# The experts' first pair read tile by tile in turn, a fixed order on TensorE, and a reordered router chain

## The chip, the core and the metric

The kernel runs on one core of one Trainium2 chip. The metric is device time in microseconds (us) of one execution; 0.2% of it is about 2.4 us. An execution that was profiled has two numbers: its own device time, and the span from its first to its last profiled instruction.

The engines are named as in the profile: PE is TensorE's matmuls, PEld its weight loads, DVE is VectorE, ACT is ScalarE, POOL is GpSimd, SP is SyncE, which here issues the large loads from HBM. SBUF is the on-chip memory that tiles are loaded into, PSUM the one that matmuls write.

## What is computed

One decoder layer for 256 tokens of width 2048, all in float32. First a mixer: RMSNorm, one wide input projection, three branches (pooling, sparse attention, cross-attention), gates and an output projection that is added to x. Then the part that matters here, a mixture of experts on the RMSNorm of the new x:

```python
lg = h @ w_router_group                      # 4 groups, top-1
le = (h @ w_router_expert).reshape(.., 4, 4) # 4 experts a group, top-2 of the chosen group
w  = pg_top * pe_top / sum(pe_top)           # from two softmaxes
a  = einsum('bsd,edf->bsef', h, w_e_gate)    # 16 experts, 2048 -> 512
b  = einsum('bsd,edf->bsef', h, w_e_up)
act = silu(a) * b * combine                  # combine is w, 0 for experts not chosen
x  = x + einsum('bsef,efd->bsd', act, w_e_down)
```

The reference multiplies every token with every expert. The kernel multiplies each expert with the tokens that chose it, up to 64 in a round; a loop after the last pair repeats the rounds where an expert has more.

## The kernel before

**Up to the residual.** The mixer takes the first 600 us and is not touched. The output projection runs in four column blocks `n` of 512; each ends in two residual tiles (token halves `t` = 0, 1) that DVE adds to `x2` (L815). `route_in` (L785 on) then transposes such a block on PE (L790), copies it to SBUF as `xt` (ACT, L792; one buffer), squares it for the norm (L793) and multiplies it with the router weights. For n < 3 these go into `rps`; for n = 3 they go straight into `rl` (L802), the PSUM tile with the 20 router values of each token.

**The router chain.** `Rc` is a copy of `rl` (L872). DVE ranks groups and experts by comparisons (L875 to L882), which gives the mask `msk`; three small matmuls (L886 to L888) count the tokens ahead of each one, and `slot` (L889) is its place with its expert. The chain of norm and softmax (`r2`, `E`, `cmb`, `cwf`, `cw`; L890 to L916) gives the weights. `warm(n, ...)` (L282) issues n matmuls of the identity whose result is not used; an f32 matmul is two instructions in the trace.

**Gathering.** Experts come in pairs (`pair(pr, ...)`, eight of them), and two pairs share one `Gather` of four experts. Its `sel` (L931) is a 0/1 matrix made from `slot`. A `step()` multiplies two 128-row blocks of x, each split into a high and a low part `xs` (ACT copy L949, DVE subtraction L950, three buffers), with `sel` (eight matmuls, L966) and DVE writes the result, scaled, to `xg` (L967). There are eight steps. `back()` transposes `sel` into `selT` for the way back and makes the factors `fac` of each token.

**A pair.** 24 weight tiles of 1 MB each: 8 of gate, 8 of up, 8 of down. `gemm` runs the 8 gate tiles into the PSUM tile `ag`, then the 8 up tiles into `au`; a tile is four f32 matmuls, eight instructions (L1006). Sigmoid (ACT) and two DVE products (L1028, L1030) give `sg`, four transposes (L1035) and a copy (L1037) give `aT`, and the eight down tiles follow (L1075), two to an output block `ad` of 512 columns. `scatter` splits `ad` into `ob` (ACT L1045, DVE L1046) and multiplies it back to the tokens with `selT` (L1051, four matmuls for both token halves); DVE adds the result to `y` (L1053). The steps of the next `Gather` are called between the tiles of the odd pair's down part; in the first pair they are called by `ahead_` in the gate gemm.

**What sets the order.** A scheduler orders each engine's instructions by a simulated timeline; `keep_in_program_order` ties one to what was traced before it on its engine. In `gemm` the first pair's gate matmuls and gather steps are tied (by `pe`, which is why the trace shows them under L991), its up matmuls are not, nor, but for `warm`, is anything else on PE in this part. SP's loads are all tied (L190), in the order of `todo`.

**The buffers of the weight tiles.** The first 18 tiles go, during the output projection, into buffers that earlier parts leave: 4 `hq` (trace name `wh`), 6 `ex` (`we`), and in turn `raw` (`wr`) and `mx` (`wm`). Two more, the tiles in `late`, go to a pool of their own once the router is done. From then on 16 buffers rotate in the fixed order hq x4, ex x6, raw, mx, raw, mx, raw, raw: each load waits until PE has finished with the tile that lay in its buffer, and all loads behind it on SP wait too. Counting loads from 0, number 20 is the first that waits for the experts' part, and number k from 36 on takes the buffer of number k - 16. Numbers 24 to 47 are pair 1, and so on; number 191 is the last tile, which is loaded in two halves.

Of the kernel before, what the change touches and what calls it, by code (L numbers as in the profile page):

```python
# [20 lines left out]
P = 128  # L21
# [32 lines left out]
def layer_kernel(tc, x, xT, memT, pos, cst, band, gains, bgate, wmem, wxq, widx, wkqvp, wpg, wgb, wo, wr, we, out):  # L54
# [671 lines left out]
    todo = deque((pr, i) for pr in range(NE // 2) for i in range(24))  # L726
    late = [(0, 6), (0, 7)]
# [55 lines left out]
    rl = sm_tile([P, NT, 20], "rl")  # L783

    def route_in(n, t, ac):  # L785
        owp = pools["ow"][1]
        sl = x2[:, t, n * 512 : (n + 1) * 512]
        ps = sm_tile([P, 4, P])
        for kk in range(4):
            nc.tensor.transpose(ps[:, kk], sl[:, kk * P : (kk + 1) * P], ident)  # L790
        xt = owp.tile([P, 4, P], F32, tag="xt", name="xt")
        A.activation(xt, ps, AF.Copy)  # L792
        A.activation(ac, sl, AF.Square, accum_out=ss2[:, t, n : n + 1])  # L793
        yield
        if n < 3:

            for kk in range(4):
                mm(rps[32 * kk : 32 * kk + 32, t * P : (t + 1) * P], wrt[:, 4 * n + kk], xt[:, kk],
                   start=n == 0 and t == 0, stop=n == 2 and t == 1)
        else:  # L800
            for kk in range(4):
                mm(rl[:, t], xt[:, kk], wrt[:, 4 * n + kk, 0:20], start=False, stop=t == 1 and kk == 3)  # L802
        yield
        if n == 2 and t == 1:
            lgT = owp.tile([P, S], F32, tag="xt", name="lgT")
            V.tensor_copy(lgT, rps)
            yield
            for u in range(NT):
                mm(rl[:, u], lgT[:, u * P : (u + 1) * P], cs[:, C_SUM : C_SUM + 20], start=u == 0, stop=False)
            yield  # L810

    for n in range(4):
        def odone(t, ac, n=n):
            sl = x2[:, t, n * 512 : (n + 1) * 512]
            V.tensor_add(sl, sl, ac)  # L815
            bg.append(route_in(n, t, ac))
# [15 lines left out]

    wps = acc_tile("warm")
    warm(7, ident, P, wps)
# [7 lines left out]
    for j, w in enumerate(late):  # L842
        et = pools["x"][1].tile([P, 4, 512], F32, name="we%d" % j)
        load(et, we[w])
        ahead.insert(w[1], et)
# [26 lines left out]
    V.tensor_copy(Rc, R.rearrange("p t g e -> p (t g) e"))  # L872
    vi = Rc.unsqueeze(3).to_broadcast(C)
    vj = Rc.unsqueeze(2).to_broadcast(C)
    V.tensor_tensor(c2, vj, vi, op=ALU.is_equal)  # L875
    V.tensor_tensor(c1, vj, vi, op=ALU.is_gt)
    V.tensor_mul(c2, c2, cs[:, C_TIE : C_TIE + 16].rearrange("p (i j) -> p i j", j=4).unsqueeze(1).to_broadcast(C))
    V.tensor_add(c1, c1, c2)
    V.tensor_reduce(rank.rearrange("p t g e -> p (t g) e"), c1, axis=AX.X, op=ALU.add)
    V.tensor_scalar(ohg, rank[:, :, 0], 0.0, None, op0=ALU.is_equal)  # L880
    V.scalar_tensor_tensor(m4[:, 0], rank[:, 0, 1:5], 1.5, ohg[:, 0].unsqueeze(2).to_broadcast([P, 4, 4]), op0=ALU.is_lt, op1=ALU.mult)
    V.scalar_tensor_tensor(m4[:, 1], rank[:, 1, 1:5], 1.5, ohg[:, 1].unsqueeze(2).to_broadcast([P, 4, 4]), op0=ALU.is_lt, op1=ALU.mult)  # L882
# [3 lines left out]
    mm(ps[:, 0], ut, msk[:, 0], start=True, stop=True)  # L886
    mm(ps[:, 1], ones, msk[:, 0], start=True, stop=False)
    mm(ps[:, 1], ut, msk[:, 1], start=False, stop=True)  # L888
    V.tensor_mul(slot, ps, msk)  # L889
# [3 lines left out]

    m1 = rt([P, NT, 5], "m1")
    tc.keep_in_program_order(V.tensor_reduce(m1, R, axis=AX.X, op=ALU.max))
# [3 lines left out]
    warm(2, ident, P, wps)  # L899
    gs = rt([P, NT], "gs")  # L900
    tc.keep_in_program_order(V.tensor_reduce(gs, E[:, :, 0], axis=AX.X, op=ALU.add))

    tc.keep_in_program_order(V.tensor_mul(cmb.rearrange("p t (g e) -> p t g e", e=4), E[:, :, 1:5], m4))
# [14 lines left out]
    gf = cs[:, C_GFFN : C_GFFN + KD]  # L918
    ys_ = []
    EQ = 4  # L920
    SQ = EQ * 64

    class Gather:

        def __init__(self, q, slot_, first=False):
            self.q = q
            self.pe = pe if first else mm
            self.sel = wk.tile([P, NT, EQ, 64], F32R, tag="sel", name="sel")  # L930
            V.tensor_tensor(  # L931
                self.sel,
                cs[:, C_IOTA : C_IOTA + 64].unsqueeze(1).unsqueeze(1).to_broadcast([P, NT, EQ, 64]),
                slot_[:, :, EQ * q : EQ * q + EQ].unsqueeze(3).to_broadcast([P, NT, EQ, 64]),
                op=ALU.is_equal)
            self.flat = self.sel.rearrange("p t e s -> p t (e s)")
            self.xg = None
            self.parts = deque()
            self.next = 0
            self.todo = deque(range(KD // 2))  # L940

        def split(self):
            if self.next == KD:
                return
            k = self.next
            self.next += 1
            xs = wk.tile([P, 2, NT, P], F32R, tag="xs", name="xs", bufs=3)
            src = x2[:, :, k * P : (k + 1) * P]
            A.activation(xs[:, 0], src, AF.Copy)  # L949
            V.tensor_sub(xs[:, 1], src, xs[:, 0])  # L950
            self.parts.append(xs)

        def step(self):
            if not self.todo:
                return
            b = self.todo.popleft()
            if self.xg is None:
                self.xg = wk.tile([P, KD, SQ], F32, tag="xg", name="xg")
            ps = sm_tile([P, 2, SQ])
            for kk in range(2):  # L960
                while len(self.parts) < 2 and self.next < KD:
                    self.split()
                xs = self.parts.popleft()
                for t in range(NT):
                    for h in range(2):
                        self.pe(ps[:, kk], xs[:, h, t], self.flat[:, t], start=t + h == 0, stop=t + h == 2)  # L966
            V.tensor_mul(self.xg[:, 2 * b : 2 * b + 2], ps, gf[:, 2 * b : 2 * b + 2].unsqueeze(2).to_broadcast([P, 2, SQ]))  # L967

        def back(self, wp):

            self.selT = wp.tile([P, 2, S], F32R, tag="selT", name="selT", bufs=2)
            ps = sm_tile([P, 2, NT, P])
            for h in range(2):
                for t in range(NT):
                    nc.tensor.transpose(ps[:, h, t], self.flat[:, t, h * P : (h + 1) * P].bitcast(F32), ident)
            A.activation(self.selT, ps.rearrange("p h t q -> p h (t q)"), AF.Copy)
            ps = sm_tile([P, 2, 18])
            for h in range(2):
                for t in range(NT):
                    for u in range(2):  # L980
                        mm(ps[:, h], self.flat[:, t, h * P : (h + 1) * P], cw[:, u, t], start=t + u == 0, stop=t + u == 2)
            self.f = wp.tile([P, 2, 2], F32, tag="fac", name="fac", bufs=2)
            for h in range(2):
                V.tensor_copy(self.f[:, h, 0:1], ps[:, h, NE : NE + 1])
                for e in range(2):
                    c = EQ * self.q + 2 * h + e
                    V.tensor_copy(self.f[64 * e : 64 * e + 64, h, 1:2], ps[64 * e : 64 * e + 64, h, c : c + 1])

    def pe(*a, **k):

        tc.keep_in_program_order(mm(*a, **k))  # L991

    def pair(pr, slot_, base, store, ga, first=False):
        hf = pr % 2

        def gemm(mm_, step=None):
            ac = acc_tile("gu")
            for i in range(8):
                if step:
                    step(i)  # L1000
                w = wtile()
                for kk in range(2):
                    k = 2 * i + kk
                    for e in range(2):
                        s0 = hf * P + 64 * e
                        mm_(ac[64 * e : 64 * e + 64], ga.xg[:, k, s0 : s0 + 64], w[:, 2 * kk + e],  # L1006
                            start=k == 0, stop=k == KD - 1)
                if i == late[-1][1] and "x" in pools:
                    close(pools.pop("x")[0])
                    pools["w2"] = pool("work2", side="right")  # L1010
            return ac

        def ahead_(i):

            while 8 - len(ga.todo) < min(8, i + 2):
                ga.step()

        ag = gemm(ga.pe if hf == 0 else mm, ahead_)
        w2 = pools["w2"][1]
        if hf == 0:  # L1020
            ga.back(w2)
        nx = ga
        if hf and not store:
            nx = Gather(pr // 2 + 1, slot_)
# [4 lines left out]
        au = gemm(mm)  # L1029
# [4 lines left out]
        for f in range(4):  # L1034
            nc.tensor.transpose(ps[:, f], sg[:, f * P : (f + 1) * P], ident)  # L1035
# [171 lines left out]
```

## Time and profile before

| | |
|---|---|
| device time, median of 3 runs | 1201.18 us (1200.85 to 1202.58) |
| the profiled execution: device time | 1201.83 us |
| the profiled execution: span | 1200.0 us |
| PE busy | 1163.4 us, 97% of the span |
| PEld / DVE / ACT busy | 66% / 48% / 35% |
| read from HBM | 337.2 MB, 201 MB of it expert weights |

A busy share is time in which some instruction of the engine was under way; matmuls overlap, so PE at 97% is not PE at its peak. Over the span the DMA engines moved 283 GB/s in the mean. PEclk is the clock granted to TensorE, 1.00 being 2.4 GHz and 0.50 being 1.2 GHz. The experts' part runs from about 717 us to the end.

### The profile page before, as it was taken

The page shows a single profiled execution, that of the slowest core. Times are in us where ns is not written, and L with a number is a line of the kernel's source. Part 1 is how long each engine was busy: PE and PEld are TensorE (multiplying, and loading weights), DVE is VectorE, ACT ScalarE, POOL GpSimd, SP SyncE. Part 2 cuts the span into 40 slices and gives each one's busy share as a digit, 9 for nine tenths or more (in the row PEclk, how much of TensorE's full clock was granted, in tenths as well). Part 3 has the DMA queues.
Part 4 walks back from the last instruction along what each step waited for, and adds up shares of the span by engine and source line. Part 5 has one row for each costly group of instructions (what it writes and reads, how often), then busy time and mean ns, then how long its engine had stood idle before and what let it go on. Part 6 is the DMA issues. An engine that isn't in the chain of part 4 may idle for free.

```text
span 1200.0 us, 14718 instructions
## 1 busy us (share of the span) xinstructions
PE 1163.4 (97%) x5855; PEld 791.5 (66%) x5855; DVE 575.7 (48%) x938; ACT 425.9 (35%) x664; POOL 30.1 (3%) x33
## 2 busy tenths in 40 slices
PE   8999999999999999999999999999999998999895
PEld 5788887888778888888887775444443544363433
DVE  7877468955465465465564434222312421141202
ACT  7765664456544444444444432201100210020000
POOL 4200000000000000000000000000000000000000
PEclk9999999999999999999999998999999999999998
DMA  9646544555555565555778475989999999999994
GB/s 384 206 147 228 176 155 170 175 176 185 202 192 204 187 215 190 206 197 209 285 289 335 167 269 203 401 345 426 375 427 426 426 426 426 427 426 426 425 426 184
DMA packets 49901, 340.34 MB, mean 284 GB/s; under 512 B 5664, under 2 KB 6304, under 8 KB 10400
## 3 DMA queue, kind: packets, MB, share of 16 engines
q1 hardware_dynamic: 46512, 329.83, 71.3%
q0 software_dynamic: 1728, 7.15, 1.7%
q10 hardware_dynamic: 1584, 2.34, 0.6%
q8 instruction: 48, 0.79, 0.3%
q14 instruction: 29, 0.24, 0.1%
HBM read 337.20 MB, written 2.10 MB: 283 GB/s over the span
## 4 chain that ended last, share of the span: by engine, by line
PE 93%; DVE 3%; ACT 2%; issue 1%; DMA 0%; DVEq 0%; ACTq 0%
PE gu L1006 18%; PE acc L269 17%; PE acc L270 17%; PE acc L268 17%; PE dn L1075 10%; PE sm L1051 3%; PE sm L966 2%; PE gu L991 1%; PE sm L991 1%; PE sm L442 1%; PE sm L686 1%; DVE wl L115 1%; ACT ob L1045 1%; DVE memT L187 1%; DVE sgm L1030 1%
## 5 line engine op out<-in xcount | busy, mean ns | idle before, releaser
L115 DVE TENSOR_TENSOR wl<-rawt,wh 128x1024 fp32r<-128x1024 f32 (+1 forms) x240 | 292.3, 1220 | 211.5 <-ACT wh L114 210.6
L114 ACT ACTIVATE wh<-rawt 128x1024 fp32r<-128x1024 f32 (+1 forms) x240 | 250.9, 1048 | 297.0 <-PE acc L270 291.4
L269 PE MATMUL acc<-wl,hT 128*128 128x512 f32 (+1 forms) x640 | 249.7, 390 | 0.7 <-DVE wl L115 0.7
L270 PE MATMUL acc<-wh,hT 128*128 128x512 f32 (+1 forms) x640 | 247.3, 387 | 0.0
L268 PE MATMUL acc<-wh,hT 128*128 128x512 f32 (+1 forms) x640 | 228.4, 390 | 0.0
L269 PEld LDWEIGHTS acc<-wl,hT 128*128 128x128 f32 x640 | 120.2, 188 | 25.1 <-DVE wl L115 1.1
L270 PEld LDWEIGHTS acc<-wh,hT 128*128 128x128 f32 x640 | 120.2, 188 | 23.1
L268 PEld LDWEIGHTS acc<-wh,hT 128*128 128x128 f32 x640 | 119.2, 188 | 23.4 <-issue 0.3
L1006 PE MATMUL gu<-we,xg 128*64 128x512 f32 x368 | 86.2, 596 | 0.0
L1045 ACT ACTIVATE ob<-dn 128x512 fp32r<-128x512 f32 (+1 forms) x33 | 19.3, 584 | 123.2 <-PE dn L1075 123.2
L1053 DVE TENSOR_TENSOR y<-y,sm 128x512 f32<-128x512 f32 (+1 forms) x58 | 36.8, 665 | 47.1 <-PE sm L1051 47.0
L1006 PE MATMUL gu<-wr,xg 128*64 128x512 f32 x240 | 58.9, 593 | 0.0
L1006 PEld LDWEIGHTS gu<-we,xg 128*64 128x64 f32 x368 | 26.0, 137 | 48.1 <-issue 44.7
L1051 PE MATMUL sm<-ob,selT 128*128 128x512 f32 (+1 forms) x132 | 45.7, 433 | 8.5 <-ACT ob L1045 8.0
L949 ACT ACTIVATE xs<-x 128x256 fp32r<-128x256 f32 x64 | 26.3, 416 | 74.7 <-PE sm L966 45.9
L269 PE MATMUL acc<-wl,mgT 128*128 128x512 f32 x128 | 51.3, 401 | 0.0
L270 PE MATMUL acc<-wh,mgT 128*128 128x512 f32 x128 | 50.7, 396 | 0.0
L1046 DVE TENSOR_TENSOR ob<-dn,ob 128x512 fp32r<-128x512 f32 (+1 forms) x33 | 22.2, 674 | 58.8 <-ACT ob L1045 58.8
L1006 PE MATMUL gu<-wh,xg 128*64 128x512 f32 x224 | 49.3, 592 | 0.0
L1075 PE MATMUL dn<-we,aT 128*64 128x256 f32 x384 | 48.2, 386 | 0.7 <-ACT aT L1037 0.7
L1030 DVE SCALAR_TENSOR_TENSOR sgm<-sgm,fac,gu 128x512 f32<-128x512 f32 x8 | 6.0, 747 | 87.8 <-PE gu L1006 87.8
L268 PE MATMUL acc<-wh,mgT 128*128 128x512 f32 x128 | 47.1, 398 | 0.0
(344 smaller groups left out, 1332.9 us busy)
## 6 DMA issues: line engine op xcount, KB each, us to landing
we<-in_we_dram SPq DMA_DIRECT2D x74, 1024.0 KB, 16.3
rawt<-in_wgb_dram SPq DMA_DIRECT2D x64, 1024.0 KB, 4.8
wh<-in_we_dram SPq DMA_DIRECT2D x48, 1024.0 KB, 15.7
wr<-in_we_dram SPq DMA_DIRECT2D x45, 1024.0 KB, 17.1
rawt<-in_wkqvp_dram SPq DMA_DIRECT2D x24, 1024.0 KB, 4.9
wm<-in_we_dram SPq DMA_DIRECT2D x24, 1024.0 KB, 15.3
rawt<-in_wo_dram SPq DMA_DIRECT2D x16, 1024.0 KB, 4.9
rawt<-in_wmem_dram SPq DMA_DIRECT2D x7, 1024.0 KB, 8.4
```

The costliest lines, as they stand in the source:

```text
L114: pin(A.activation(hi, ps, AF.Copy))
L115: pin(V.tensor_sub(lo, ps, hi))
L268: mm(o, hi[:, c], wh[:, kk], start=f, stop=False)
L269: mm(o, hi[:, c], wl[:, kk], start=False, stop=False)
L270: mm(o, lo[:, c], wh[:, kk], start=False, stop=l)
L949: A.activation(xs[:, 0], src, AF.Copy)
L966: self.pe(ps[:, kk], xs[:, h, t], self.flat[:, t], start=t + h == 0, stop=t + h == 2)
L1006: mm_(ac[64 * e : 64 * e + 64], ga.xg[:, k, s0 : s0 + 64], w[:, 2 * kk + e], start=k == 0, stop=k == KD - 1)
L1045: A.activation(ob[:, 0], ad, AF.Copy)
L1051: mm(ps, ga.selT[:, hf, t * P : (t + 1) * P], ob[:, u], start=u == 0, stop=u == 1)
L1053: V.tensor_add(ys, base(t)[:, c0 : c0 + n], ps)
L1075: mm(ad[64 * e : 64 * e + 64, 256 * i : 256 * i + 256], aT[:, k, 64 * e : 64 * e + 64], w[:, k, 256 * e : 256 * e + 256], start=k == 0, st ...
```

## The change

- In the first pair, tile i of gate and tile i of up are used in turn, and loaded in this order (`use`); the late tiles are the last of each, (0, 7) and (0, 15).
- All matmuls and transposes from the last residual block on are tied to program order (`pe`, `turn`).
- The last scatter of a pair is left open and done behind the first gate tile of the next pair (`finish` there).
- The router: the n = 3 blocks are transposed one behind the other, with two `xt` buffers and three warm matmuls between; 14 (before 7) warm matmuls follow the router's, and 4 (before 2) the slot matmuls; the squares come behind the copies. The first three `xs` parts are made by DVE alone and, tied, stand before the ranking; the first gather step stands before the norm and softmax chain; `sel` is made in two halves.
- `factors` (8 small matmuls) is cut out of `back` and stands behind the gate part (first pair: before the last two tiles); `back` stands before the up part (first pair: behind it); the gather steps of a pair with a new `Gather` start behind its up part, as before.

```diff
-    todo = deque((pr, i) for pr in range(NE // 2) for i in range(24))
-    late = [(0, 6), (0, 7)]
+    use = [(0, i + 8 * j) for i in range(8) for j in range(2)] + [(0, i) for i in range(16, 24)]
+    use += [(pr, i) for pr in range(1, NE // 2) for i in range(24)]
+    todo = deque(use)
+    late = [(0, 7), (0, 15)]
...
-        xt = owp.tile([P, 4, P], F32, tag="xt", name="xt")
+        xt = owp.tile([P, 4, P], F32, tag="xt", name="xt", bufs=2)
...
+    def pe(*a, **k):
+        i = mm(*a, **k)
+        tc.keep_in_program_order(i)
+        return i
+    def turn(ps, src):
+        tc.keep_in_program_order(nc.tensor.transpose(ps, src, ident))
+    rl = rl_[0]
+    xts = []
+    for t in range(NT):
+        ps = sm_tile([P, 4, P])
+        for kk in range(4):
+            turn(ps[:, kk], x2[:, t, (12 + kk) * P : (13 + kk) * P])
+        xt = pools["ow"][1].tile([P, 4, P], F32, tag="xt", name="xt", bufs=2)
+        pin(A.activation(xt, ps, AF.Copy))
+        xts.append(xt)
     wps = acc_tile("warm")
-    warm(7, ident, P, wps)
+    warm(3, ident, P, wps)
+    for t in range(NT):
+        for kk in range(4):
+            pe(rl[:, t], xts[t][:, kk], wrt[:, 12 + kk, 0:20], start=False, stop=t == 1 and kk == 3)
+    for t in range(NT):
+        pin(A.activation(last[t], x2[:, t, 3 * 512 :], AF.Square, accum_out=ss2[:, t, 3:4]))
+    warm(14, ident, P, wps)
...
+    def part(k, dve=False):
+        xs = wk.tile([P, 2, NT, P], F32R, tag="xs", name="xs", bufs=3)
+        src = x2[:, :, k * P : (k + 1) * P]
+        if dve:
+            pin(V.tensor_copy(xs[:, 0], src))
+            pin(V.tensor_sub(xs[:, 1], src, xs[:, 0]))
...
+    parts0 = [part(k, True) for k in range(3)]
+    pin(V.tensor_copy(Rc, R.rearrange("p t g e -> p (t g) e")))
...
+    warm(4, ident, P, wps)
+    pin(V.tensor_mul(slot, ps, msk))
...
+    ga = Gather(0, slot, parts0)
+    ga.step()
+    inorder.clear()
...
+        ag, au = acc_tile("gu"), None
+        if pr == 0:
+            au = acc_tile("gu")
             for i in range(8):
+                gathered(i + 2)
+                if i == 7:
+                    ga.factors()
+                use_tile(ag, i)
+                use_tile(au, i)
...
+        else:
+            for i in range(8):
+                gathered(8)
+                use_tile(ag, i)
+                finish()
+            if hf == 0:
+                ga.factors()
+            elif not store:
+                nx = Gather(pr // 2 + 1, slot_)
+                nx.split(3)
...
+        if hf == 0:
+            ga.back(w2)
+        if au is None:
+            au = acc_tile("gu")
+            for i in range(8):
+                use_tile(au, i)
         V.scalar_tensor_tensor(sg, sg, c1s, au, op0=ALU.mult, op1=ALU.mult)
         if nx is not ga:
             nx.step()
...
             if not (store and n == 3):
                 emit(ad, n * 512, 512)
-        finish()
+        if store:
+            finish()
         return nx
```

## Rows read from the trace of the kernel before

**Rows 1.** Waits of PE from 760 us on: engine, line, waited for: us, times, longest.

```profile
PE sm L1051 <- ACT ob L1045: 8.0, 11, 0.8
PE sm L1035 <- DVE sgm L1030: 7.1, 8, 0.9
```

**Rows 2.** SP in order of time: start us, us, queue, line, load, count.

```profile
733.29 16.73 SPq L190 DMA_DIRECT2D wh<-in_we_dram  x4
...
1094.59 7.68 SPq L190 DMA_DIRECT2D wh<-in_we_dram  x4
...
1133.88 7.67 SPq L190 DMA_DIRECT2D wh<-in_we_dram  x4
...
1160.99 2.71 SPq L190 DMA_DIRECT2D wm<-in_we_dram  x2
```

**Rows 3.** DMA issues from 733 and from 1160 us: count, KB each, us to landing.

```profile
wh<-in_we_dram SPq DMA_DIRECT2D x4, 1024.0 KB, 5.0
...
wm<-in_we_dram SPq DMA_DIRECT2D x2, 512.0 KB, 18.7
```

**Rows 4.** Windows: stretch and length, busy us by engine, PEclk, DMA share, GB/s.

```profile
728.00:732.00 4.00, 4.00 (x19) 3.38 (x20) 3.48 (x14) 1.75 (x5) 0.00 (x0) 0.57 0.01 2
...
884.00:888.00 4.00, 2.61 (x14) 0.85 (x10) 0.75 (x1) 0.41 (x1) 0.00 (x0) 1.00 1.00 424
...
920.00:960.00 40.00, 39.15 (x239) 19.89 (x236) 12.91 (x25) 6.79 (x15) 0.00 (x0) 1.00 1.01 426
```

**Rows 5.** All engines in order of time, 717 to 731 us: start us, us, instruction.

```profile
719.17 0.98 PE L802 MATMUL rl<-wrt,xt 128*128 128x20 f32 x8
...
720.89 1.64 PE L802 MATMUL rl<-wrt,xt 128*128 128x20 f32 x8 [0.75 <-ACT xt L792]
...
722.36 3.33 PE L282 MATMUL warm<-ident 128*128 128x128 f32 x14
722.57 0.20 DVE L872 COPY wrt<-rl 128x40 f32<-128x40 f32 x1 [0.94 <-PE rl L802]
722.64 0.20 POOL L851 MEMSET ones<- 128x128 bf16 x1 [165.13 <-PE rl L802]
...
723.49 0.41 DVE L950 TENSOR_TENSOR xs<-x,xs 128x256 fp32r<-128x256 f32 x1
...
725.84 0.17 DVE L882 SCALAR_TENSOR_TENSOR msk<-wrt,ohg 128x16 bf16<-128x16 f32 x1
...
727.41 3.88 PE L991 MATMUL sm<-sel,xs 128*128 128x256 f32 x16
```

**Rows 6.** PE in order of time, the first pair's gate and up part.

```profile
731.22 2.03 PE L991 MATMUL gu<-wh,xg 128*64 128x512 f32 x8
...
733.50 1.94 PE L1006 MATMUL gu<-we,xg 128*64 128x512 f32 x8
735.37 0.74 PE L991 MATMUL sm<-sel,xs 128*128 128x256 f32 x4
```

**Rows 7.** The chain that ended last, in order of time: start us, us, what.

```profile
772.88 0.76 DVE sgm L1030
...
775.03 7.12 PE dn L1075 x62
782.15 0.67 PE sm L1051 x2
...
826.04 0.76 DVE sgm L1030
...
860.95 25.07 PE gu L1006 x116
...
939.27 0.76 DVE sgm L1030
```

**Rows 8.** All engines in order of time, the last tile and the last sum.

```profile
1186.17 1.95 PE L1075 MATMUL dn<-wm,aT 128*64 128x256 f32 x16 [0.50 <-DVE ob L1046]
...
1190.04 0.75 DVE L1053 TENSOR_TENSOR y<-y,sm 128x256 f32<-128x256 f32 x2 [0.48 <-PE sm L1051]
```

More of the change, by code (lines that the diff above doesn't have):

```diff
@@ L844, in layer_kernel @@
         load(et, we[w])
-        ahead.insert(w[1], et)
+        ahead.insert(use.index(w), et)
     def rt(shape, name):
@@ L884, in layer_kernel @@
+    pin(V.tensor_add(c1, c1, c2))
+    pin(V.tensor_reduce(rank.rearrange("p t g e -> p (t g) e"), c1, axis=AX.X, op=ALU.add))
+    pin(V.tensor_scalar(ohg, rank[:, :, 0], 0.0, None, op0=ALU.is_equal))
+    for t in range(NT):
+        pin(V.scalar_tensor_tensor(m4[:, t], rank[:, t, 1:5], 1.5, ohg[:, t].unsqueeze(2).to_broadcast([P, 4, 4]),
+                                   op0=ALU.is_lt, op1=ALU.mult))
     slot = rt([P, NT, NE], "slot")
     ps = sm_tile([P, NT, NE])
-    mm(ps[:, 0], ut, msk[:, 0], start=True, stop=True)
@@ L887, in layer_kernel, with __init__, split, step @@
-    mm(ps[:, 1], ones, msk[:, 0], start=True, stop=False)
-    mm(ps[:, 1], ut, msk[:, 1], start=False, stop=True)
-    V.tensor_mul(slot, ps, msk)
+    pe(ps[:, 0], ut, msk[:, 0], start=True, stop=True)
+    pe(ps[:, 1], ones, msk[:, 0], start=True, stop=False)
+    pe(ps[:, 1], ut, msk[:, 1], start=False, stop=True)
+    warm(4, ident, P, wps)
+    pin(V.tensor_mul(slot, ps, msk))
+    class Gather:
+        def __init__(self, q, slot_, parts=()):
+            self.q = q
+            self.sel = wk.tile([P, NT, EQ, 64], F32R, tag="sel", name="sel")
+            for t in range(NT):
+                pin(V.tensor_tensor(
+                    self.sel[:, t],
+                    cs[:, C_IOTA : C_IOTA + 64].unsqueeze(1).to_broadcast([P, EQ, 64]),
+                    slot_[:, t, EQ * q : EQ * q + EQ].unsqueeze(2).to_broadcast([P, EQ, 64]),
+                    op=ALU.is_equal))
+            self.flat = self.sel.rearrange("p t e s -> p t (e s)")
+            self.xg = None
+            self.parts = deque(parts)
+            self.next = len(self.parts)
+            self.todo = deque(range(KD // 2))
+        def split(self, n):
+            while len(self.parts) < n and self.next < KD:
+                self.parts.append(part(self.next))
+                self.next += 1
+        def step(self):
+            if not self.todo:
+                return
+            b = self.todo.popleft()
+            if self.xg is None:
+                self.xg = wk.tile([P, KD, SQ], F32, tag="xg", name="xg")
+            ps = sm_tile([P, 2, SQ])
+            for kk in range(2):
+                self.split(1)
+                xs = self.parts.popleft()
+                for t in range(NT):
+                    for h in range(2):
+                        pe(ps[:, kk], xs[:, h, t], self.flat[:, t], start=t + h == 0, stop=t + h == 2)
+            V.tensor_mul(self.xg[:, 2 * b : 2 * b + 2], ps, gf[:, 2 * b : 2 * b + 2].unsqueeze(2).to_broadcast([P, 2, SQ]))
+            self.split(3)
+        def back(self, wp):
+            self.selT = wp.tile([P, 2, S], F32R, tag="selT", name="selT", bufs=2)
+            ps = sm_tile([P, 2, NT, P])
+            for h in range(2):
+                for t in range(NT):
+                    turn(ps[:, h, t], self.flat[:, t, h * P : (h + 1) * P].bitcast(F32))
+            A.activation(self.selT, ps.rearrange("p h t q -> p h (t q)"), AF.Copy)
+        def factors(self):
+            ps = sm_tile([P, 2, 18])
+            for h in range(2):
+                for t in range(NT):
+                    for u in range(2):
+                        pe(ps[:, h], self.flat[:, t, h * P : (h + 1) * P], cw[:, u, t], start=t + u == 0, stop=t + u == 2)
+            self.f = wk.tile([P, 2, 2], F32, tag="fac", name="fac", bufs=2)
+            for h in range(2):
+                V.tensor_copy(self.f[:, h, 0:1], ps[:, h, NE : NE + 1])
+                for e in range(2):
+                    c = EQ * self.q + 2 * h + e
+                    V.tensor_copy(self.f[64 * e : 64 * e + 64, h, 1:2], ps[64 * e : 64 * e + 64, h, c : c + 1])
@@ L989, in pe @@
[L989 to L997, printed above, removed]
-            for i in range(8):
[L999 to L1018, printed above, removed]
-        w2 = pools["w2"][1]
[L1020 to L1024, printed above, removed]
+    open_ = deque()
@@ L1111, in layer_kernel @@
     reg = nc.values_load(nri[0:1, 0:1], min_val=0, max_val=S // CAP - 1)
-    todo.extend((pr, i) for pr in range(NE // 2) for i in range(24))
+    todo.extend(use)
     with tc.For_i(0, reg):
```

142 lines of the change are left out of this document (49 added, 93 removed).

## The prediction

> **What bounds the kernel now.** I read the waits of PE first. From 760 us on PE waits 8.0 us for ACT's `ob` (11 times) and 7.1 us for DVE's last product (8 times), and for no DMA at all [rows 1]. So the order of the work on PE ends each stage, not the weights. Then I looked how far the weights are behind. SP's rows give their pace: 16 loads of 1 MB were issued from 1094.59 to 1133.88, 2.456 us each [rows 2], at 426 GB/s [rows 4]. The last load was out by 1163.70 and took 18.7 us to land, against 5.0 for a load with nothing ahead of it [rows 2, 3]: about 1182, and PE begins that tile at 1186.17 [rows 8]. So the stream of weights ends only 4 us ahead of its use. Two pairs take PE 113.2 us (826.04 to 939.27, both the end of an odd pair's up part [rows 7]) and the stream 48 x 2.456 = 117.9. The stream is the slower of the two; it is not yet the bound because it starts with 20 tiles in hand. A gain on PE alone would therefore be worth 4 us and no more; it counts if the stream comes forward too. It can: in the first pair SP issued four loads in 16.7 us [rows 2], and the DMA engines stood at 0.01 from 728 to 732 [rows 4].
>
> **The change part by part.** I follow PE to the start of pair 1, then the stream from there.
>
> *Router.* The n = 3 router matmuls began at 719.17, behind the transposes, and the second eight waited 0.75 us for the one `xt` buffer, then ran at a falling clock, to 722.5 [rows 5]. Two buffers remove the wait. Three warm matmuls (6 instructions) come in: 14 took 3.33 us at half clock, 0.24 each, so 0.12 at full clock, 0.7 us. Sixteen router instructions at 0.98 / 8 make 2.0 us. They end at 721.8.
>
> On DVE the ranking took from 722.57 to 726.01 with three subtractions of 0.41 between [rows 5]; without them 2.2 us. But three copies and three subtractions now stand, tied, before it. A copy of this shape within SBUF is not shown; below it lies the small copy of 0.20, and the subtraction of the same shape, 0.41, is the nearest row, which I take: 6 x 0.41 = 2.5 us. When may they start? `ones`, the first tile of the work pool, waited for the router matmuls [rows 5], so the pool's first tiles lie where `xt` lay. `xs` was late in that pool and is now sixth, so I expect its first buffer there too, under one of the two `xt`: the copies wait until that half's router matmuls are done (720.9) and end at 723.4. Then the mask is ready at 725.6, only 0.4 us earlier than before. If nothing is shared they end before 721.8 and the mask comes at 724.0. The Trainium skill (VectorE: DVE Perf Modes, The perf-mode tier table) has an f32 copy between SBUF tiles at twice the pace of a two-tensor operation; by that the three copies would be some 0.4 us shorter in all and the sum below 0.4 us less.
>
> The 28 warm instructions end at 721.8 + 28 x 0.12 = 725.2, just in time, at full clock. From mask to gather were 1.4 us (726.01 to 727.41); `sel` in halves saves 0.3; the four warm matmuls end with it. Two steps took 3.81 us at half clock (16 matmuls from 727.41 to 731.22 [rows 5, 6]), so 1.9 at full clock. With 0.3 for the parts that are refilled, the first gate tile starts at 729.0 instead of 731.22. Norm and softmax chain, squares and `xg` lie beside 30 us of gate and up work and cost nothing; without that cover the chain would stand before `factors`.
>
> *First pair.* A tile in an unbroken run costs 25.07 / 116 x 8 = 1.73 us [rows 7], alone between others 1.87 (733.50 to 735.37 [rows 6]). Sixteen tiles with eight breaks: 28.8. A gather step of eight lies between 0.95 (half of 1.9) and 1.48 (twice the 0.74 of four [rows 6]); 1.2 taken, six left: 7.2. `factors`, eight small matmuls like the router's: 1.0. Together 37.0, so the up part ends at 766.0; before it ended at 772.88, after 41.7 us. From there to the down part 2.15 us (772.88 to 775.03 [rows 7]); the sigmoid and first product now have only the last up tile (1.73) as cover, which about holds; if not, 0.8 more, a product's time. Eight down tiles at 7.12 / 62 x 16 = 1.84 and three scatters at 2 x 0.67 [rows 7]: 18.7. Pair 1 starts at 766.0 + 2.15 + 18.7 = 786.9.
>
> *The stream.* In the first pair buffers now come free in the order in which SP wants them, two in 2 x 1.73 + 0.14 + 1.2 = 4.8 us, the stream's own pace. Loads 34 to 39 wait for down tiles, at 2.3 to 3.1 us, so no queue is left by load 40, which waits for pair 1's first tile (786.9 + 1.95) and lands 5.0 later, at 794. From there buffers come free every 1.73 us and the stream runs unbroken. The tightest place is load 63, which waits for the last down tile of pair 1: 786.9 + 27.7 + 1.3 = 815.9, then 8 x 1.84 + 3 x 1.34 + 8 x 1.2 + 0.7 = 29.0, so it lands at 850 or later, where the stream would have it at 794 + 23 x 2.456 = 850.5. The remaining 151 tiles take 370.9: the last half lands at 1164.9.
>
> *Later pairs on PE.* Two pairs: 32 x 1.73 + 16 x 1.84 + 8 x 1.34 + 8 x 1.2 + 2.15 + 2.9 for transposes and factors = 110.1. Against 113.2 that is the `ob` waits gone (a whole down tile now lies between a block and its scatter) and some broken runs mended. PE then ends the last up tile at 815.9 + 3 x 110.1 = 1146.2 and the last down tile at 1146.2 + 2.15 + 14.7 + 4.0 = 1167.1; the stream permits 1164.9 + 0.95 (half of the last tile's 1.95) = 1165.9. The two limits meet; my PE prices credit no overlap, so I take the stream.
>
> *End.* From the last tile's end (1188.12) to the last sum's (1190.79) were 2.7 us [rows 8], and 9.2 more to the span's end at 1200.0. 1165.9 + 2.7 + 9.2 = 1177.8. The profiled execution took 1.8 us more than its span and 0.65 more than the median of the runs: **1179**.
>
> **Rivals.**
> (a) PE stays the bound. The tied order gives nothing in the later pairs, because a step at the head of PE's queue waits for its part (an ACT copy and a DVE subtraction, 0.8 us, behind `ob` and `y` work) and all matmuls wait behind it. Only the first pair's 10 us (826.04 to 815.9) remain: 1191; with 0.8 us at five steps of each odd pair, 1195. For: the scheduler's order had no wait in odd pairs but DVE's product. Against: a down tile of 1.84 us lies between two steps.
> (b) The clock falls in the router, as it did before: at 728 to 732 it is still 0.57 [rows 4], and what PE did ahead of the fall were transposes and matmuls of 20 columns. The 28 warm instructions then take 6.7 us from 722.5 and the gate starts at about 733.4. All shifts by 4.4: 1183.5. Against: the warm matmuls now stand between the transposes and the router's; and from 884 to 888, with PE busy for 2.61 of 4 us, the clock stayed at 1.00 [rows 4].
> (c) Slower: PE now outruns the stream, waits at every tile, and the clock is halved for it. A gate tile then takes 3.46 us, more than the stream's 2.456, and PE bounds at half clock: 1.0 us a tile more. Over pairs 6 and 7 (48 tiles) that makes 1179 + 48 = 1227; it is slower than before from 22 such tiles on. Against: a waiting PE would still work 1.73 of 2.46 us, a larger share than that of 884 to 888. The Trainium skill (TensorE: Matmul & The Clock Gate, HAM oscillation) describes this fall, matmuls that wait for a DMA at each tile and start each at the low clock; in its case the waits were longer than the work, and no run here shows it.
> (d) It does not do what it says. The scheduler already put up tiles among the gate tiles [rows 6], and tied work can lose elsewhere what it gains. If PE kept 41.7 us in the first pair, 1184; if nothing came forward, 1201.
>
> **How the numbers follow.** Forecast 0.60 (1174 to 1184, from `xs` unshared, -1.5, and a late sigmoid or late refills, +4); (a) 0.15, (b) 0.13, (c) 0.07, (d) at no gain 0.05. The range 1172 to 1194 takes in (a)'s lower end and (b) and leaves out (c), (d) and a tail below. Measured here, 0.2% or 2.4 us is what can be told from no change. Faster: 0.60 + 0.15 + 0.13 = 0.88; same 0.05; slower 0.07.
>
> **What would show it.** First gate matmul near 729 with PEclk 1.00 from 717 on; the first pair's up part done near 766; DMA near 426 GB/s from 735 to 765 and unbroken from about 790 on; the three `ob` waits of even pairs gone; and, new, PE waiting for DMA in the last pairs. Wrong would be: PE without such waits at the end (then (a)), a clock of 0.5 after 721 (b) or late in the run (c), or DMA gaps after 800.

## The result and the profile after

The changed kernel takes 1192.2 us (1191.94 to 1193.62) against 1201.0 for the kernel before in the same runs: 0.9927 of it, 95% interval 0.9910 to 0.9944. That is 8.8 us faster where 22 were forecast, and inside the range. The profiled execution has a span of 1190.4 us, where the forecast had 1177.8. One execution of tied_alone (below) took 1943.8 us at a mean granted clock of 0.555 and is left out of that run's ratio.

The waits of PE from 760 us on, in the changed kernel (engine, line, waited for: us, times, longest), answer to [rows 1]:

```profile
PE sm L847 <- DVE sgm L1092: 5.9, 5, 2.5
PE gu L842 <- DMA wh<-in_we_dram: 4.4, 8, 0.6
PE dn L842 <- ACT aT L1099: 3.4, 5, 0.7
PE gu L842 <- DMA wr<-in_we_dram: 3.0, 6, 0.6
PE gu L842 <- DMA we<-in_we_dram: 1.5, 3, 0.5
PE gu L842 <- DMA wm<-in_we_dram: 1.4, 3, 0.5
```

The 8.0 us for ACT's `ob` are gone, and 10.3 us of waits for weights of the gate and up parts have come in 20 pieces, all from pair 5 on. So the weights seem to end the kernel now; the delays below test it. The windows (stretch, length, busy us of PE, PEld, DVE, ACT, POOL, PEclk, DMA share, GB/s) show where the stream is whole and where it is not:

```profile
728.00:732.00 4.00, 2.65 (x16) 1.67 (x17) 2.58 (x10) 2.71 (x7) 0.00 (x0) 1.00 0.02 6
735.00:765.00 30.00, 30.00 (x156) 13.48 (x157) 8.86 (x24) 5.53 (x13) 0.00 (x0) 1.00 0.99 403
765.00:772.00 7.00, 4.01 (x22) 1.56 (x18) 2.30 (x5) 2.49 (x4) 0.00 (x0) 1.00 0.83 352
772.00:777.00 5.00, 4.79 (x30) 2.90 (x32) 0.00 (x0) 0.16 (x1) 0.00 (x0) 0.66 0.13 21
777.00:790.00 13.00, 13.00 (x100) 7.87 (x98) 5.21 (x8) 1.79 (x3) 0.00 (x0) 1.00 0.78 276
790.00:1150.00 360.00, 346.17 (x2010) 160.83 (x2008) 95.22 (x186) 43.26 (x86) 0.00 (x0) 1.00 1.01 424
```

At 728 to 732 the clock is 1.00 (it was 0.57 in [rows 4]). From 790 to 1150 the DMA share is 1.01 in the mean. But between 765 and 790 there is a hole in the stream, where loads wait for their buffers, and in it the clock falls: PEclk is 0.66 in the mean of 772 to 777. PE in order of time shows why (start us, us, instruction, wait):

```profile
764.14 3.65 PE L842 MATMUL gu<-we,xg 128*64 128x512 f32 x16
767.73 0.66 PE L847 MATMUL sm<-ident,sel 128*128 128x128 f32 x4
770.89 0.63 PE L847 MATMUL sm<-ident,sgm 128*128 128x128 f32 x4 [2.51 <-DVE sgm L1092]
772.21 3.06 PE L842 MATMUL dn<-wr,aT 128*64 128x256 f32 x16 [0.69 <-ACT aT L1099]
775.04 2.53 PE L842 MATMUL dn<-wm,aT 128*64 128x256 f32 x16
```

and DVE in the same stretch:

```profile
768.42 0.76 DVE L949 TENSOR_TENSOR sel<-cs,slot 128x256 fp32r<-128x256 f32 x2 [3.38 <-PE sm L847]
769.21 0.75 DVE L1085 SCALAR_TENSOR_TENSOR sgm<-gu,fac,sgm 128x512 f32<-128x512 f32 x1
770.00 0.75 DVE L1092 SCALAR_TENSOR_TENSOR sgm<-sgm,fac,gu 128x512 f32<-128x512 f32 x1
```

The `sel` at 768.42 is the second Gather's, which pair 1 needs. The scheduler put it ahead of pair 0's two products. It waits for the transposes at 767.73, the last readers of the one `sel` buffer, which the change has put behind the up part; the products wait behind it on DVE, and PE's transposes of `sgm` behind them. After that idle time the first two down tiles run at a fallen clock.

SP in order of time (start us, us, queue, line, load, count) answers to [rows 2]:

```profile
763.26 0.33 SPq L190 DMA_DIRECT2D wm<-in_we_dram  x1
775.30 4.37 SPq L190 DMA_DIRECT2D wr<-in_we_dram  x2
784.06 8.08 SPq L190 DMA_DIRECT2D wh<-in_we_dram  x4
793.82 10.18 SPq L190 DMA_DIRECT2D we<-in_we_dram  x6
```

Counting loads from the first as 0, 763.26 is load 33, 775.30 load 34 and 793.82 load 40. That one took 7.3 us to land by the DMA issues from 793 us (count, KB each, us to landing), not the 5.0 of a free queue [rows 3]:

```profile
we<-in_we_dram SPq DMA_DIRECT2D x1, 1024.0 KB, 7.3
```

So it landed at 801.16, and from there SP's queue was never empty until the last load.

### The profile page after: what moved, and what is told of

It is laid out like the page before. It is cut to its first block, busy times and chain, and to the rows that moved or that the text cites. A ratio compares the mean times of both kernels' runs of the same rounds, so it can differ in the third digit from the quotient of the medians.

```text
span 1190.4 us, 14757 instructions
## 1 busy us (share of the span) xinstructions
PE 1150.9 (97%) x5879; PEld 789.1 (66%) x5879; DVE 575.2 (48%) x945; ACT 424.6 (36%) x661; POOL 30.2 (3%) x33
## 4 chain that ended last, share of the span: by engine, by line
## 5 line engine op out<-in xcount | busy, mean ns | idle before, releaser
L270 PEld LDWEIGHTS acc<-wh,hT 128*128 128x128 f32 x640 | 120.2, 188 | 23.2
L842 PE MATMUL gu<-we,xg 128*64 128x512 f32 x400 | 89.8, 596 | 1.5 <-DMA we<-in_we_dram 1.5
L842 PE MATMUL gu<-wh,xg 128*64 128x512 f32 x256 | 58.0, 596 | 4.4 <-DMA wh<-in_we_dram 4.4
L842 PE MATMUL gu<-wr,xg 128*64 128x512 f32 x240 | 56.2, 596 | 3.0 <-DMA wr<-in_we_dram 3.0
L842 PEld LDWEIGHTS gu<-wh,xg 128*64 128x64 f32 x256 | 17.5, 137 | 42.5 <-issue 30.3
```

What stands on the lines that cost most here:

```text
L270: mm(o, lo[:, c], wh[:, kk], start=False, stop=l)
L842: i = mm(*a, **k)
```

## The experiments

All are against the kernel before, each in its own group of runs (its median was 1200.9 to 1201.5 in them); 1192.2 is the changed kernel. "Load 40" is its landing in the profiled execution, and "rest" the time from there to the end of the last instruction. The twelve kernels of the table with PE's later order tied have a rest of 387.9 to 389.9 us, wherever load 40 lands. no_warm stands further down, as its profiled execution was not like its others.

| run | time, us | ratio, 95% interval | load 40 | rest |
|---|---|---|---|---|
| changed kernel | 1192.2 | 0.9927 (0.9910 to 0.9944) | 801.16 | 389.2 |
| sel_tied | 1188.2 | 0.9889 (0.9874 to 0.9904) | 797.49 | 389.1 |
| exp_tied | 1190.7 | 0.9912 (0.9899 to 0.9926) | 800.33 | 388.6 |
| both_tied | 1186.9 | 0.9880 (0.9865 to 0.9895) | 796.36 | 389.7 |
| gate_then_up | 1188.9 | 0.9899 (0.9885 to 0.9914) | 798.40 | 388.6 |
| delay_pair1 | 1195.1 | 0.9952 (0.9939 to 0.9966) | 803.30 | 389.9 |
| delay_pair4 | 1191.6 | 0.9920 (0.9907 to 0.9934) | 802.06 | 389.4 |
| scatter_at_end | 1193.8 | 0.9938 (0.9927 to 0.9950) | 804.57 | 388.7 |
| tied_alone | 1194.5 | 0.9942 (0.9929 to 0.9955) | 803.53 | 389.4 |
| late_mid | 1187.3 | 0.9881 (0.9866 to 0.9896) | 797.64 | 387.9 |
| stores_behind | 1186.0 | 0.9872 (0.9857 to 0.9887) | 796.29 | 387.9 |
| late_and_stores | 1186.4 | 0.9870 (0.9855 to 0.9885) | 796.61 | 388.0 |
| later_untied | 1200.0 | 0.9990 (0.9982 to 0.9999) | 805.08 | 392.8 |

**The two waits ahead of the hole.** sel_tied:

```diff
-                pin(V.tensor_tensor(
+                tc.keep_in_program_order(V.tensor_tensor(
                     self.sel[:, t],
```

> As the changed kernel, with the two halves of each later Gather's sel tied behind what stands before them on DVE, so that the scheduler no longer puts them between factors and the first product of pair 0. Theory A (from pair 1 on the weights' stream sets the end, so what PE saves before pair 1's first tile comes out whole): the down part of pair 0 starts 2.3 us earlier (2.15 after the up part in place of 4.42), the clock does not fall at 772.9 (1.7 us more), pair 1 starts at about 787.9, the time falls from 1192.2 to about 1188.2. Rival B (loads 34 to 39 would then queue behind each other, and the stream swallows the clock's part): 1190. Rival C (the end is set by PE or by waits in the later pairs): 1192.

1188.2, as theory A had it. PE in this kernel:

```profile
767.77 0.66 PE L847 MATMUL sm<-ident,sel 128*128 128x128 f32 x4
768.69 0.66 PE L847 MATMUL sm<-ident,sgm 128*128 128x128 f32 x4 [0.27 <-DVE sgm L1092]
770.03 1.95 PE L842 MATMUL dn<-wr,aT 128*64 128x256 f32 x16 [0.69 <-ACT aT L1099]
771.81 1.90 PE L842 MATMUL dn<-wm,aT 128*64 128x256 f32 x16
```

The wait of 2.51 has become 0.27, and the two down tiles take 1.95 and 1.90 in place of 3.06 and 2.53. The clock does not fall (the columns of the windows above):

```profile
770.00:777.00 7.00, 6.97 (x58) 4.40 (x60) 1.38 (x2) 0.60 (x1) 0.00 (x0) 1.00 0.61 213
```

Load 40 landed 3.7 us earlier and the time fell by 4.0.

exp_tied:

```diff
-        A.activation(E[:, t], E[:, t], AF.Exp, scale=r2[:, t : t + 1])
+        tc.keep_in_program_order(A.activation(E[:, t], E[:, t], AF.Exp, scale=r2[:, t : t + 1]))
```

> As the changed kernel, with the softmax's Exp tied behind the two ACT copies that refill xs, so that its table load (1.28 us) no longer stands ahead of them. Theory A: the two waits of the second gather step (0.81 and 0.54 us) shrink to under 0.3 together, the first gate tile starts near 729.2 in place of 731.2, the time falls by 2.0 to 1190.2. Rival C: no change, 1192. A third possibility: the copies wait for something else (the xs buffers), and the gate tile starts at 731 as before.

1190.7: 1.5 of the 2.0, within the spread of its five runs (1189.0 to 1192.0), so the time alone does not show it; load 40 landed 0.8 us earlier. The two waits in the changed kernel, ahead of its first gate tile (PE):

```profile
727.24 1.69 PE L842 MATMUL sm<-sel,xs 128*128 128x256 f32 x12
729.74 0.38 PE L842 MATMUL sm<-sel,xs 128*128 128x256 f32 x1 [0.81 <-ACT xs L915]
730.66 0.62 PE L842 MATMUL sm<-sel,xs 128*128 128x256 f32 x3 [0.54 <-DVE xs L916]
731.21 1.08 PE L842 MATMUL gu<-wh,xg 128*64 128x512 f32 x4
```

ACT had the table load first there:

```profile
727.58 1.28 ACT L1016 ACT_TABLE_LOAD   x1 [6.42 <-DVE r L147]
728.87 0.51 ACT L1016 ACTIVATE wrt<-wrt,r 128x20 f32<-128x20 f32 x2
729.29 1.01 ACT L915 ACTIVATE xs<-x 128x256 fp32r<-128x256 f32 x3
```

With the tie the copies start at 728.17, and PE's wait for ACT is gone. The first gate tile moved by 1.0 only, from 731.21 to 730.21, since DVE then has `xg` ahead of the subtraction (DVE in exp_tied, then PE):

```profile
728.59 0.69 DVE L978 TENSOR_TENSOR xg<-sm,cs 128x512 f32<-128x512 f32 x1 [0.80 <-PE sm L842]
729.20 0.75 DVE L916 TENSOR_TENSOR xs<-x,xs 128x256 fp32r<-128x256 f32 x2
```

```profile
729.67 0.61 PE L842 MATMUL sm<-sel,xs 128*128 128x256 f32 x3 [0.53 <-DVE xs L916]
```

both_tied has both edits.

> Both ties. Theory A: the savings add, pair 1 starts at about 785.9, 1186.2. Rival B: 1188 to 1189. Rival C: 1192.

1186.9, between A and B: pair 1 started at 787.02, 1.1 later than A had it, by the `xs` wait that stayed.

**Is it the stream from load 40 on?** delay_pair1 and delay_pair4 put this into pair 1 or pair 4, ahead of its gate tiles:

```diff
+            if pr == 1:
+                for _ in range(21):
+                    pe(ag[:, :P], ident, ident, start=True, stop=True)
```

> As the changed kernel, with 21 matmuls of 128 columns (5.0 us at full clock, by 0.24 us each in the router's warm run) put on PE ahead of the first gate tile of pair 1; their sums are overwritten. Theory A: load 40 is issued 5 us later, and all of it comes out at the end: 1197.2. Rival C, or a stream that has slack here: 1192 to 1194.

> As the changed kernel, with the 21 matmuls (5.0 us) of delay_pair1 ahead of the first gate tile of pair 4 instead. Theory A (the stream sets the end, and from load 88 on SP has eight loads queued, each landing 19.6 us after its issue): the delay is hidden, 1192.2 to 1193. Rival C (PE's own pace in the later pairs still counts): up to 1197.

In pair 4 the 5 us vanish (1191.6). In pair 1 they cost 2.9 by the medians, not 5.0: load 40 was issued 4.6 us later (798.44) but landed only 2.1 later, in 4.9 us (row of delay_pair1):

```profile
we<-in_we_dram SPq DMA_DIRECT2D x1, 1024.0 KB, 4.9
```

So in the changed kernel load 40 already stands in a queue of some 2.4 us, built up by loads 36 to 39. What counts whole is time won ahead of load 34, where the stream stands empty; at pair 1's first tile about half of it counts (2.1 on the landing, 2.9 in the time), and at pair 4 nothing.

**Which part of the change brings the gain?** later_untied takes the tie of PE's order away after pair 0 (of the transposes too, which the cut leaves out):

```diff
-        tc.keep_in_program_order(i)
+        if not free:
+            tc.keep_in_program_order(i)
...
             nri = rounds()
+            free.append(True)
```

> As the changed kernel, with PE's order from pair 1 on left to the scheduler again (pair 0 stays tied). Theory A: two pairs take PE up to 113.2 us as in the kernel before, in place of 107.0; pairs 5 to 7 hold some 15 us of waits for the stream, so most of 3 x 6.2 is hidden: 1192 to 1195. Rival G (the tied order of the later pairs is itself worth its 6 us a pair of pairs): 1200 or more.

1200.0, rival G. Its waits of PE from 760 on are those of [rows 1] again, and none is for a DMA:

```profile
PE sm L850 <- DVE sgm L1097: 8.5, 8, 2.5
PE sm L842 <- ACT ob L1112: 8.0, 11, 0.8
PE dn L842 <- ACT aT L1104: 3.4, 5, 0.7
```

Theory A had misjudged the cover: the waits for the stream that I counted as room exist only because PE is fast there. From its end of pair 1's up part (824.37) PE needs three times 112.9 us to that of pair 7 (1162.95), against 1157.21 with the tie, and its last down part takes 21.2 us in place of 19.1. But that is not 6 us in each pair of pairs, as rival G has it: of the 7.9 us by which the last down tile ends later, 3.6 are lost by 824.37 already (820.80 with the tie), 2.2 in the three pairs of pairs and 2.1 in the last down part. The first loss is at the change to pair 1, where PE takes two gate tiles ahead of pair 0's last down tile (PE in later_untied):

```profile
789.68 3.60 PE L842 MATMUL gu<-we,xg 128*64 128x512 f32 x14
795.53 1.95 PE L842 MATMUL dn<-wh,aT 128*64 128x256 f32 x16
```

So load 39, which waits for that tile, is issued at 797.52 in place of 791.82, and load 40 lands 3.9 us later.

tied_alone is the other half: the kernel before, with its router and first pair as they were, and the order tied from pair 1 on (the cut leaves out the scatter that is carried to the next pair and the parts split ahead).

```diff
+    def pl(*a, **k):
+        i = mm(*a, **k)
+        if tied:
+            tc.keep_in_program_order(i)
...
-        au = gemm(mm)
+        au = gemm(pl)
...
             nri = rounds()
+            tied.append(True)
```

> The kernel before, with its router and its first pair left as they are, and only PE's order from pair 1 on tied as in the changed kernel (with the last scatter of a pair behind the next pair's first gate tile, and a Gather's parts split three ahead). Theory H (the end is the later of two limits: the stream, 389 us from load 40's landing to the end of the span as in the changed kernel's profile, 801.16 to 1190.4, and PE's own order): load 40 lands near 803 as before, so 803 + 389 is a span of 1192, 1194 in all; the tied order alone brings 7 of the 9 us, the early part 2. Rival I (both parts are needed, as each limit alone holds the time): 1199 or more.

1194.5: theory H to half a microsecond. PE waits for weights again:

```profile
PE gu L926 <- DMA wh<-in_we_dram: 4.4, 8, 0.6
PE sm L931 <- DVE sgm L1057: 4.2, 5, 0.9
PE dn L926 <- ACT aT L1064: 3.4, 5, 0.7
PE gu L926 <- DMA wr<-in_we_dram: 2.9, 6, 0.6
```

So the order of the later pairs, with the carried scatter and the parts split ahead, is worth 6.4 of the 8.8 us alone. The earlier start is worth 2.3 on top of it by the medians; the intervals of the two overlap, but load 40 lands 2.4 us earlier. Without the order the early part brings about 1, since later_untied loses its gain again ahead of load 40.

gate_then_up undoes the in-turn order of pair 0 alone:

```diff
-    use = [(0, i + 8 * j) for i in range(8) for j in range(2)] + [(0, i) for i in range(16, 24)]
-    use += [(pr, i) for pr in range(1, NE // 2) for i in range(24)]
+    use = [(pr, i) for pr in range(NE // 2) for i in range(24)]
...
-    late = [(0, 7), (0, 15)]
+    late = [(0, 6), (0, 7)]
...
-                use_tile(ag, i)
-                use_tile(au, i)
+                use_tile(ag, i)
```

> As the changed kernel, with pair 0's eight gate tiles ahead of its eight up tiles, loads in that order and the two late tiles at (0, 6) and (0, 7), as in the kernel before; PE's order stays tied. Theory A (PE's pace to pair 1 counts, and the in-turn order gave nothing itself but put sigmoid, product and back behind the up part): the same 36.6 us for gate and up, 2.15 to the down part in place of 4.42 and no fall of the clock, pair 1 starts near 788, 1188.2 as in sel_tied. Rival F (the in-turn order is what brought the gain, since only it frees two buffers each 4.8 us from the start): the gate part is slowed by its gather steps or the stream starts later, 1195 or more.

1188.9, theory A: 3.3 us faster than the changed kernel. Gate and up took 37.3 us (36.6 in turn), and the down part began 2.2 after them, since the transposes of `sel` and the sigmoid then lie under the up tiles. The in-turn order, one of the three things in the title, is a loss as it stands; with the `sel` tied (1188.2, intervals overlapping) it is level with gate ahead of up.

scatter_at_end empties the open scatter at each pair's end (`finish()` without `if store`).

> As the changed kernel, with the last scatter of each pair again at that pair's end, ahead of the next pair's first gate tile. PE then waits for ob there (8.0 us over 11 waits in the kernel before, and 1.2 us of scatter ahead of the tile). Theory A: only pair 0's counts, about 2 us by which pair 1's first tile frees its buffer later, of which the queue at load 40 swallows half, as it did in delay_pair1: 1193. Rival G: all eight count, 1200.

1193.8 (1191.2 to 1196.6): 1.6 us above the changed kernel by the medians, with overlapping intervals; rival G's 1200 is excluded. PE waits for `ob` ahead of pair 1 (0.70 and 0.23 us), and load 40 lands 2.5 us later than in delay_pair4, which is the same kernel up to pair 4. I take delay_pair4 for this because PEclk was 0.50 from 772 to 777 in both profiles, while it was 0.66 in the changed kernel's: the fall behind the 2.5 us wait is not the same in each execution. The times of the kernels with that wait spread over 1.7 to 5.4 us, those of the other kernels of the table over 0.5 to 1.8; that the fall is the reason was not tested.

no_warm leaves out the router's three `warm` calls.

> As the changed kernel, without the 21 warm matmuls of the router (3, 14 and 4 of them). If they keep the clock: it falls to half during the ranking, the two gather steps take 3.8 us in place of 1.9 and the first gate tiles begin at half clock, S at 733 to 734, all of it ahead of load 34, so 1194.5 to 1196. If the clock stays up without them: S at 731 or 0.7 earlier, 1191.5 to 1192.

1195.4 (ratio 0.9954, 0.9941 to 0.9966), four of five runs at 1194.8 to 1196.1. The fifth, which was the profiled one, took 1190.8, so its rows don't show what the others paid. Even in it the clock fell:

```profile
720.00:724.00 4.00, 1.29 (x12) 1.19 (x11) 2.96 (x16) 1.39 (x5) 0.49 (x2) 0.94 0.97 410
724.00:728.00 4.00, 1.48 (x9) 1.45 (x10) 3.58 (x23) 0.32 (x1) 0.00 (x0) 0.50 0.80 334
728.00:732.00 4.00, 3.73 (x18) 2.48 (x19) 2.43 (x10) 2.81 (x7) 0.00 (x0) 0.71 0.01 2
```

There it was back at 1.00 by 732 and the first gate tile began at 731.0. What the others lost is not shown in rows; their mean granted clock was 0.987, against 0.991 in the profiled one. Over some 1190 us that is about 10 us more at half clock, an estimate from these two means, so the clock is the likely cause. The 3.2 us between the medians are not clear of noise: the two intervals touch.

**What is left after both ties.** late_mid, on top of both_tied:

```diff
-    late = [(0, 7), (0, 15)]
+    late = [(0, 4), (0, 12)]
```

> As both_tied, with the two tiles that have no buffer of the ring put at (0, 4) and (0, 12) in place of (0, 7) and (0, 15), so that the last gate and up tile of pair 0 free a ring buffer each. Theory A2 (after both_tied the end is set by the hole in the stream between loads 33 and 36, whose buffers come free only with the down part's tiles; in both_tied the loads 34 to 40 land 3.0 to 5.1 us apart in place of 2.456): the hole moves to a place where the queue is some 4 us deep and is absorbed there, load 34 is issued near 766 in place of 771.06, load 40 lands near 790 in place of 796.36, the time falls from 1186.9 to about 1181. Rival D (the hole is as long wherever it stands): load 40 lands at 796 again and the time stays at 1187.

1187.3: rival D, and my reasoning was at fault. Fourteen ring buffers come free in the gate and up part wherever the two other tiles stand, so load 34 is always the one that waits for the first down tile (issued at 771.29 as at 771.06). Loads 34 to 36 still landed 3.7, 3.9 and 4.9 us behind the load before them (4.3, 3.5 and 5.1 in both_tied), and a second hole came at loads 28 and 29 (5.0 and 3.9).

stores_behind, on top of both_tied (the last pair's loads are written ahead of its down part, so that SP has no store in front of a load):

```diff
-                    nc.scalar.dma_start(out[t * P : (t + 1) * P, c0 : c0 + n], ys)
+                    q = nc.scalar if n < 512 else nc.sync
+                    q.dma_start(out[t * P : (t + 1) * P, c0 : c0 + n], ys)
```

> As both_tied, with the output stores of columns 0 to 1535 issued by SP on the queue of the weights, so behind its last load, in place of ACT's own queue. Theory A2 (four of these 256 KB stores, 1 MB, go between the last weights, so that loads 183 to 192 take 22.9 us in place of the 19.65 of eight at 2.456): the last half load lands near 1170.9 in place of 1173.3, the stores land after it beside PE's last tile, the time falls to about 1184.5. Rival E (the stores land later and end the kernel, or the last loads are slow for another reason): 1187 to 1189.

> As both_tied, with both edits, the late tiles at (0, 4) and (0, 12) and the first output stores behind the weights. If both theories hold the savings add: 1178.6. If only the late tiles count 1181, if only the stores 1184.5.

1186.0 and 1186.4, 0.5 to 0.9 below both_tied with overlapping intervals: not told apart, and far from the 2.4 expected. The mechanism shows in the last two half loads (DMA issues from 1150, first both_tied, then stores_behind):

```profile
wm<-in_we_dram SPq DMA_DIRECT2D x2, 512.0 KB, 20.7
```

```profile
wm<-in_we_dram SPq DMA_DIRECT2D x2, 512.0 KB, 17.7
```

The last one landed at 1169.90 in place of 1173.31, but PE's last down tile ended only 2.0 earlier, for PE was now late itself. In stores_behind it ran without a wait from 1154.55 to the end of that tile:

```profile
1167.52 1.94 PE L842 MATMUL dn<-wr,aT 128*64 128x256 f32 x16
1169.38 1.21 PE L842 MATMUL sm<-ob,selT 128*128 128x512 f32 x4
1170.53 1.95 PE L842 MATMUL dn<-wm,aT 128*64 128x256 f32 x16
```

stores_behind has the lowest median here, 6 us below the changed kernel; both_tied, simpler and not told apart from it, gives 5 of them.

## Why the prediction was right and wrong

The end was right: with PE's order tied, the weights set it, as delay_pair4 and the constant rest show. What a gain on PE alone is worth was wrong (below), and so were several sizes. These add up, but for rounding, to the 12.6 us by which the span (1190.4) missed 1177.8:

| step of the prediction | forecast | measured | miss |
|---|---|---|---|
| first gate tile | 729.0 | 731.21 | +2.2 |
| pair 0's gate and up | 37.0 | 36.6 | -0.4 |
| from there to the down part | 2.15 | 4.42 | +2.3 |
| down part, to pair 1's first tile | 18.7 | 19.6 | +0.9 |
| pair 1's first tile to load 40's landing | 7.0 | 9.3 | +2.3 |
| load 40 to load 183, 143 tiles | 351.2 | 354.1 | +2.9 |
| load 183 to the last tile's end | 20.7 | 23.2 | +2.5 |
| from there to the end | 11.9 | 11.9 | 0.0 |

- **The step that failed most** is "from there to the down part 2.15 us": I asked what covers the sigmoid and the product, not what stands ahead of them on DVE. The clock's fall that followed (some 1.7 us on two tiles) is in the row below it, so they cost 4.0 us, and sel_tied gave back 4.0. The later place of `back` makes the wait, the scheduler's free placing of `sel` puts the product behind it; gate_then_up, which removes the first, gains nearly as much (3.3).
- **"A gain on PE alone would therefore be worth 4 us and no more"** failed too. tied_alone is such a gain: load 40 lands there as before (803.53, before 803.20), and the time falls by 6.4. PE's untied order had also held back the stream: in the kernel before, loads 63 and 65, which wait for pair 1's last down tile and pair 2's second gate tile, landed 4.4 and 5.0 us behind the load before them; in tied_alone no load behind 40 lands more than 3.6 behind the one before. From load 40 to load 183 it took 357.7 us before and 355.0 in tied_alone. So a faster PE brought the later part of the stream forward by itself, and nothing had to come earlier in the first pair for it.
- **"0.3 for the parts that are refilled"** was 1.35 (0.81 for ACT's copy behind Exp's table load, 0.54 for DVE's subtraction). exp_tied shows the first. The rest of the 2.2 us: the sixteen gather matmuls took 2.7 us of PE at a clock of 1.00, not half of 3.8, and began at 727.24, 0.5 later than the 726.7 of the prediction. The three copies took 0.28 us each where 0.41 was taken.
- **"So no queue is left by load 40"** was wrong. Loads 36 to 39 came free faster than they landed, and load 40 landed in 7.3 us; delay_pair1, where the queue was gone, has 4.9.
- **The pace** of 2.456 us came from rows without a stall. Over 143 tiles it was 2.476: most lie 2.41 to 2.51 apart, six 2.8 to 3.4 (load 43 and 113 the most). The cause of these six is open.
- **"The stream permits 1165.9"** took half a tile from the last landing. But when the stream feeds the last up tile (load 183), PE has the whole down part still ahead: 1145.2 + 2.0 + 2.15 + 18.7 makes 1168.1 by the prediction's own prices. PE's line beside it (1146.2 for the last up tile) was reckoned without waits for the stream. From 1166 on the first output stores went between the last weights. Between both_tied and stores_behind that is 3.4 us on the landing and 2.0 on PE; in the changed kernel it is at most some 1.1 on PE (23.2 us against the 22.1 of stores_behind, which has no wait).

The working of the later pairs held: two pairs take PE 107.0 us (820.80 to 927.81), priced 110.1, before 113.2. "The two limits meet" held in a sharper form than I gave it: later_untied and tied_alone show that PE's order was the limit that had to go first. The prediction spent its length on the early part, which brings about 1 us without the order and about 2 on top of it.

Of the rivals, (a) did not come: from 760 us on PE waits for no `xs`. Its upper price was also summed wrongly: 0.8 us at five steps are 4 us in each of three odd pairs with a new `Gather`, so 1203 and not 1195. What a PE that stays the bound looks like later_untied shows, in a kernel whose first pair is early: 1200.0, where 1191 carried pair 0's gain through; `ob` and product waits stayed in all later pairs. (b) did not come: the clock was 1.00 from 717 to 732; no_warm, without the matmuls that are to hold it, has 0.50 at 724 to 728 and a median 3.2 us higher, which is not clear of noise. (c) did not come: with 17 waits of some 0.5 us for weights the clock stood at 1.00 from 790 to 1150. The fall that the Trainium skill describes (TensorE: Matmul & The Clock Gate, HAM oscillation) is therefore not seen at waits of 0.5 us in each 2.45; the one fall between the router and the last tile, at 772 to 777, followed 2.5 us of idle time. (d) was true of the in-turn order alone.

## What to carry to other kernels

Before an instruction is moved later, list what the scheduler has queued behind its result on each engine: a buffer's next writer may stand ahead of work that is urgent, and one pinned instruction then returns more than the move gave. Where two limits lie within a few microseconds, take each away alone before crediting a part of the change: here the part with the long working was worth 2 us and the tie 6. Against a stream, time won counts whole only ahead of the point where the stream runs dry, and count the buffers that come free, not their order.

## What the runs showed of the hardware

- One core moved weights at 424 GB/s for 360 us with the DMA share at 1.01 (790 to 1150 in the changed kernel), and at 426 from 810 to 1150 in every other kernel of the experiments.
- Output stores on ACT's queue took their share from loads already queued on SP's: both_tied's two last half loads landed in 20.7 us, 17.7 in stores_behind, with the stores on the weights' own queue behind them.
- The granted clock stood at 1.00 while PE waited 0.5 us in each 2.45 us for weights. After 2.5 us of idle time between two groups of four transposes PEclk was 0.66 in the mean of 772 to 777; in sel_tied, with 0.27 us in its place, it was 1.00 from 770 to 777.
